# Spreading the last norm's rows in four quarters, and seeding both final row halves ahead of the last scatters, in a hybrid MoE kernel

## The chip, the cores and the metric

The kernel runs on one core of one Trainium2 chip. The metric is device time in microseconds (us), the median of a few runs. One further execution was taken by the hardware profiler; all rows below come from it. The engines are named as in the profile: PE (TensorE matmuls), PEld (its weight loads), DVE (VectorE), ACT (ScalarE), POOL (GpSimd), SP (SyncE, which issues the weight DMAs).

## What is computed

Two layers over 256 tokens of width 1024, float32. Layer 0 mixes tokens by a Conformer convolution, layer 1 by chunkwise retention with four heads. After each mixer comes a mixture of experts (MoE) in which every token goes to two of 32 experts of one chosen group. Every sub-layer is followed by a norm:

```python
for i in range(DEPTH):                       # DEPTH = 2
    mix = conformer_conv(x, ...) if i % 2 == 0 else retention(x, positions, ...)
    x = layer_norm(DEEPNORM_ALPHA * x + mix, ln1_g[i], ln1_b[i])
    ffn = hier_moe(x, ...)                   # sum over e of combine[:, e] * (silu(x @ w_gate[e]) * (x @ w_up[e])) @ w_down[e]
    x = layer_norm(DEEPNORM_ALPHA * x + ffn, ln2_g[i], ln2_b[i])
```

All 32 experts' weights (1024x512 twice and 512x1024 once per expert) are read in each layer, whatever the routing.

## The kernel before

**Stages.** Convolution, MoE of layer 0, retention, MoE of layer 1, output. In an MoE stage `experts` runs over 32 experts `e` and, inside each, over four steps `i` (0 to 3); a place in it is written (e, i) here. `gate_up(e, i)` multiplies the expert's gathered 64 token slots with a quarter of its gate and up weights: four matmuls, 8 records in the trace, since a matmul with fp32 operands leaves two records. `hidden(e)` after (e, 3) makes silu(gate) times up, on ACT and DVE. `turn(e)` transposes that on PE (tile `hT`). `down(es, kt)` multiplies with a quarter of the down weights of a pair of experts (tile `y`, again 8 records). `parts` scales and splits the result into a high and a low fp32r part (`yh`, `yl`), `places` builds the 0/1 matrix that puts slots back on tokens (`sp`, `s`), and `scatter` adds a pair's result to the tokens: eight one-pass matmuls, two token halves `tt` by two column halves `n` by high and low. For most pairs DVE then adds the PSUM tile to the tokens in `cur`.

**The end of a stage.** The last pairs are not added by DVE. `begin(tt)` seeds two PSUM tiles `fin` with `cur` itself, by a matmul of the identity with `cur` in fp32 operands, and the last scatters accumulate onto them; the norm then reads `fin`. Before, `begin(0)` stands at (30, 3) and `begin(1)` at (31, 3); the scatter of pair 14 at (31, 2) therefore goes into `fin` for token half 0 alone, and through DVE for half 1. Experts 30 and 31 are handled singly (numbers -2 and -1 in tile names).

**The norm's rows.** The last norm needs its scale and shift on all 128 partitions. `spread_rows` makes them from a 32-row tile `lnr`: 16 matmuls, each broadcasting one column of the identity, into four PSUM tiles, each copied out by ACT. Before, all four are made at one place, `ROWS_AT = (29, 0)`, after `run(29, 0)`.

**The order.** The order on every engine is the order of the code. The table `plan`, filled by `planned(e, q, ...)`, says which of down, turn, parts, place, scatter, begin follow the gate/up group at (e, q). `Weights` streams 1 MB weight pieces through a ring of SBUF tiles: SP issues a piece when a tile is free and an earlier transfer has landed. Within an expert the pieces come as gate and up (first half), down pieces where the plan has them, gate and up (second half).

**PSUM.** Eight tiles of 512 columns: four of tag `acc` (`acc1`: gate/up and down results), four of tag `sm` (`sm1`: transposes, gathers, places, scatters, rows, `fin`).

Of the kernel before, what the change touches and what calls it, by code (L numbers as in the profile page):

```python
# [10 lines left out]
F32 = mybir.dt.float32  # L11
F32R = mybir.dt.float32r
BF = mybir.dt.bfloat16
I32 = mybir.dt.int32
AF = mybir.ActivationFunctionType
OP = mybir.AluOpType
AX = mybir.AxisListType

P = 128
D = 1024  # L20
T = 256
KT = 8
DEPTH = 2
NE = 32
# [8 lines left out]
ONCE = {7: "split", 16: "hand", 17: "hand"}  # L33
T4 = 9
SPLIT = 4
ROWS_AT = (29, 0)
WARM = [11, 8, 8, 0, 2, 0, 1, 2]
YB = 2
TAPS_PE = [2, 2, 2, 2, 2, 2, 2, 14]
# [4 lines left out]
RW = 2 * DEPTH * KT  # L44
# [142 lines left out]
def trunk(ctx, tc, a, out):  # L187
    nc = tc.nc
    ET = mybir.EngineType
    V, S, G, PE = nc.vector, nc.scalar, nc.gpsimd, nc.tensor  # L190
# [15 lines left out]
    def sm1(name, dt=F32):  # L206
        return psum.tile([P, 512], dt, tag="sm", name=name, bufs=4)
# [10 lines left out]
    def planned(e, q, *steps):  # L218
        plan.setdefault((e, q), []).extend(steps)


    for p in range(NE // 2 - 1):
        e, both = 2 * p + 2, (2 * p, 2 * p + 1)
        planned(e - 1, 0, ("turn", e - 2))
        planned(e, 0, ("turn", e - 1))
        planned(e, 2, ("down", both, 0))
        planned(e, 3, ("down", both, 1))
        planned(e + 1, 0, ("down", both, 2))
        planned(e + 1, 1, ("down", both, 3), ("parts", p), *([("place", -2)] if p == NE // 2 - 2 else []))
        if p < NE // 2 - 2:  # L230
            planned(e + 2, 0, ("scatter", p))
    z = NE - 1
    planned(z - 1, 3, ("begin", 0))
    planned(z, 0, ("turn", z - 1))
    planned(z, 2, ("down", (z - 1,), 0), ("scatter", NE // 2 - 2), ("down", (z - 1,), 1), ("place", -1))
    planned(z, 3, ("begin", 1), ("down", (z - 1,), 2), ("down", (z - 1,), 3), ("part", -2), ("turn", z),
            *[("down", (z,), k) for k in range(4)], ("ahead", 2), ("part", -1), ("ahead", 4), ("scatter", -2),
            ("scatter", -1))

# [41 lines left out]
    lnr = consts.tile([RW, P], F32, name="lnr")  # L281
# [7 lines left out]
    part = cc[:, 259:260]  # L289
# [16 lines left out]
    ident = consts.tile([P, P], F32, name="ident")  # L306
# [13 lines left out]
    def cut(t):  # L320
        return [t[:, n:n + 512] for n in range(0, t.shape[1], 512)]
# [1 line left out]
    def row_bcast(src, n):  # L323
        return bass.AP(tensor=src.tensor, offset=src.offset, ap=[[0, P], [1, n]])

    def spread_rows(L, o):

        for n in range(4):
            ps = sm1(f"row{L}{n}")
            for k in range(4):  # L330
                q = L * 2 * KT + n * 4 + k
                PE.matmul(ps[:, k * P:(k + 1) * P], ident[:RW, q:q + 1].to_broadcast([RW, P]), lnr, start=True, stop=True)
            S.activation(o[:, n * 512:(n + 1) * 512], ps, AF.Copy)

    def layer_stats(tt, halves, name):
        st = small.tile([P, 2, 6], F32, tag="bst", name=name + "st")
# [306 lines left out]
    def halves(tt):  # L643
        return [cur[:, tt, n * 512:(n + 1) * 512] for n in range(2)]
# [286 lines left out]
    def moe(L, prev, next_front):  # L931
        with tc.tile_pool(name=f"moe{L}", bufs=1) as mp:
            x1h = mp.tile([P, 2, KT, P], F32R, tag="x1h", name="x1h")
            x1l = mp.tile([P, 2, KT, P], F32R, name="x1l")
            comb = mp.tile([P, 2, NE], F32, name="comb")
            posm = mp.tile([P, 2, NE], F32, name="posm")
            posT = mp.tile([NE, T], BF, name="posT")
            flag = mp.tile([1, 1], I32, name="flag")
            W.open(mp)
            with tc.tile_pool(name=f"exp{L}", bufs=1) as ep:  # L940
                norms(*prev, moe_front(L, x1h, x1l))
                W.more()
                route(L, ep, mark["lg"], comb, posm, posT, flag)
                fin = experts(L, mp, ep, x1h, x1l, comb, posm, posT, flag)
                W.room.update(own=0, split=0)
                norms([fin[0], fin[1]], *mark["ln2"], f"lnm{L}", next_front(), 4)
# [91 lines left out]
    def experts(L, mp, ep, x1h, x1l, comb, posm, posT, flag):  # L1038
# [91 lines left out]

        def places(pr):

            sp = sm1(f"sp{pr}")
            for j in range(2):
                e = 2 * pr + j if pr >= 0 else NE + pr
                PE.matmul(sp[j * CAP:(j + 1) * CAP, :T], identb[:NE, e:e + 1].to_broadcast([NE, CAP]), posT,  # L1136
                          start=True, stop=True)
            s0[pr] = ep.tile([P, T], F32R, tag="s0", name=f"s0{pr}", bufs=2)
            V.tensor_scalar(s0[pr], sp[:, :T], slot, None, op0=OP.is_equal)  # L1139
# [10 lines left out]
        def scatter(pr, on=None):  # L1150

            for tt in range(2):
                for n in range(2):
# [6 lines left out]
                    if not held:  # L1160
                        o = halves(tt)[n]
                        V.tensor_tensor(o, ps, o, op=OP.add)  # L1162

        def begin(tt):
            fin[tt] = [sm1(f"fin{tt}{n}") for n in range(2)]
            for n in range(2):
                PE.matmul(fin[tt][n], ident, halves(tt)[n], start=True, stop=False)

        def run(e, q):
            for what, *step in plan.get((e, q), ()):  # L1170
                if what == "down":
                    down(*step)
                elif what == "turn":
                    turn(*step)
                elif what == "begin":
                    begin(*step)
                elif what == "parts":
                    places(*step)
                    parts(*step)
                elif what == "place":  # L1180
                    places(*step)
                elif what == "part":
                    parts(*step)
                elif what == "ahead":
                    W.stop = len(pieces)
                    W.ahead(*step, pool=step[0] > 2)
                else:
                    scatter(*step, fin)

        def extra():  # L1190
# [5 lines left out]
            pair = [acc1(f"ov{n}") for n in range(2)]  # L1196
            with tc.If(rv > 0):
                overflow(L, x1h, x1l, comb, posm, wts, big, mid, row, pair)
        fin = {}
        W.stop = layers[L][1]  # L1200
        one_hots(0)
        warm(WARM[5])
# [2 lines left out]
        for e in range(NE):  # L1205
            for i in range(4):
                gate_up(e, i)
                if e == 0 and i == 0:
                    gather(0, range(2, 4))
                    turned()  # L1210
                if e == 0 and i == 3:
                    extra()
                    W.used(2)
                    for tt in range(2):
                        S.activation(cur[:, tt], cur[:, tt], AF.Copy, scale=ALPHA)
                if i == 3:
                    hidden(e)
                run(e, i)
                if e + 4 < NE and e % 4 == 1 and i == 0:
                    one_hots(e // 4 + 1)  # L1220
                if e + 2 < NE and e % 4 == 2:
                    gather(e // 4 + 1, [i])
                if (e, i) == ROWS_AT:
                    rows = mp.tile([P, 2048], F32, tag="x1h", name=f"rows{L}")
                    spread_rows(L, rows)
            if L == 0 and e == 3:
                mark["rot"] = rotary_tables()
            if L == 0 and e == 10:
                mark["rot"]()
        rows = cut(rows)  # L1230
# [74 lines left out]

    moe(0, conv(), ret_front)
    moe(1, retention(), out_front)


# [59 lines left out]
```

## Time and profile before

| | us |
|---|---|
| timed runs, median (lowest to highest) | 1306.99 (1303.9 to 1308.12), 3 runs |
| profiled execution, device time | 1302.16 |
| profiled execution, span of the trace | 1300.4 |
| PE busy in the span | 1253.6 (96%) |
| DVE / ACT / POOL busy | 488.2 / 334.3 / 139.4 |

PE's busy share includes records whose ends are modelled, and a matmul that stalls on weights is drawn stretched, so 96% is not 96% of useful work. Times in the rows are from the span's start. "xN" is the number of records merged in a row; what stands in brackets is the idle time of that engine just before the row and what ended it.

### The profile page before, as it was taken

What the parts mean: (1) busy time and instruction counts of PE and PEld (TensorE: products, weight loads), DVE (VectorE), ACT (ScalarE), POOL (GpSimd) and SP (SyncE); (2) the same over time, 40 slices, a digit from 0 to 9 for tenths busy, and PEclk for the clock granted to TensorE, in tenths of its full rate; (3) what the DMA queues carried; (4) which work ended last, traced back from release to release, by engine and by line L of the source; (5) the groups of instructions that cost most, each with busy time, mean ns of one, the idle gap of its engine ahead of it and who ended that gap; (6) DMA issues with size and microseconds to landing.
All of it is one profiled execution on the core that took longest, in us unless ns stands there. A gap on an engine that the chain in (4) does not pass through costs nothing.

```text
span 1300.4 us, 15536 instructions
## 1 busy us (share of the span) xinstructions
PE 1253.6 (96%) x6163; PEld 662.8 (51%) x6163; DVE 488.2 (38%) x859; ACT 334.3 (26%) x553; POOL 139.4 (11%) x165
## 2 busy tenths in 40 slices
PE   9989899999999999998999999899999999999996
PEld 7867444343443434434997788544443444434432
DVE  5987322223222222126666755413222232222224
ACT  4655321121111112113433543311111111111111
POOL 4881009100000000003130000000000000000000
PEclk9999799999999999999999999799999999999998
DMA  9935699999999999999655565699999999999992
GB/s 322 392 127 176 231 385 427 426 424 426 425 426 426 425 426 426 425 426 407 234 191 181 174 209 199 239 382 420 418 425 426 424 427 426 426 425 424 426 427 83
DMA packets 102391, 459.45 MB, mean 353 GB/s; under 512 B 8259, under 2 KB 25443, under 8 KB 59555
## 3 DMA queue, kind: packets, MB, share of 16 engines
q1 hardware_dynamic: 102082, 457.92, 87.3%
q8 instruction: 53, 0.87, 0.2%
q0 software_dynamic: 80, 0.26, 0.1%
q10 hardware_dynamic: 144, 0.15, 0.1%
q14 instruction: 32, 0.25, 0.1%
HBM read 457.25 MB, written 1.05 MB: 352 GB/s over the span
## 4 chain that ended last, share of the span: by engine, by line
PE 47%; DMA 38%; DVE 2%; ACT 1%; issue 0%; DVEq 0%; SPq 0%; ACTq 0%
DMA w<-in_moe_w_up_dram 21%; PE gu L1071 15%; DMA w<-in_moe_w_down_dram 14%; PE y L1126 7%; PE gp L1057 3%; DMA w<-in_moe_w_gate_dram 2%; PE vg L790 2%; PE vg L788 2%; PE vg L789 2%; PE sc L1158 2%; PE qk L771 1%; PE qk L770 1%; PE qk L768 1%; PE wo L656 1%; PE wo L657 1%; PE wo L658 1%
## 5 line engine op out<-in xcount | busy, mean ns | idle before, releaser
L1071 PE MATMUL gu<-w,xghi 128*64 128x512 f32 x1024 | 256.0, 614 | 2.6 <-DMA w<-in_moe_w_up_dram 1.4
L1126 PE MATMUL y<-w,h 128*64 128x512 f32 x960 | 240.4, 596 | 10.8 <-DMA w<-in_moe_w_down_dram 10.8
L1071 PE MATMUL gu<-w,xglo 128*64 128x512 f32 x1024 | 242.4, 599 | 0.0
L1082 DVE TENSOR_TENSOR h<-gl,gu 64x512 f32<-64x512 f32 x64 | 67.8, 1059 | 364.5 <-ACT gl L1080 364.5
L1126 PEld LDWEIGHTS y<-w,h 128*64 128x64 f32 x960 | 73.1, 138 | 156.9 <-issue 136.5
L1071 PEld LDWEIGHTS gu<-w,xglo 128*64 128x64 f32 x1024 | 70.1, 137 | 119.5 <-issue 110.9
L1071 PEld LDWEIGHTS gu<-w,xghi 128*64 128x64 f32 x1024 | 68.6, 139 | 114.0 <-issue 103.7
L143 DVE TENSOR_TENSOR l<-w,h 128x1024 fp32r<-128x1024 f32 x66 | 83.6, 1270 | 68.5 <-ACT h L142 66.9
L1080 ACT ACTIVATE gl<-gu 64x512 f32<-64x512 f32 x64 | 37.7, 589 | 243.7 <-PE gu L1071 243.6
L142 ACT ACTIVATE h<-w 128x1024 fp32r<-128x1024 f32 x72 | 75.7, 1058 | 88.1 <-PE vg L790 31.7
L1104 ACT ACTIVATE h<-hT 128x256 f32<-128x256 f32 x64 | 24.6, 385 | 270.8 <-PE hT L1101 153.7
L1162 DVE TENSOR_TENSOR cur<-sc,cur 128x512 f32<-128x512 f32 x116 | 72.1, 684 | 23.3 <-PE sc L1158 23.3
L1113 DVE COPY gsl<-hT 64x1 f32<-64x1 f32 x60 | 9.4, 156 | 174.6 <-ACT h L1104 174.1
L1057 PE MATMUL gp<-oh,x1h 128*128 128x256 f32 x256 | 59.0, 313 | 3.5 <-DVE route L1010 3.5
L1146 ACT ACTIVATE yh<-y,gsl 128x512 fp32r<-128x512 f32 x60 | 41.2, 687 | 80.5 <-PE y L1126 80.4
L1057 PEld LDWEIGHTS gp<-oh,x1h 128*128 128x128 f32 x256 | 40.5, 196 | 40.3 <-issue 39.3
L466 PE MATMUL pw<-xT,w 128*128 128x256 f32 x256 | 57.8, 381 | 1.6 <-DMA w<-in_conv_w_pw_dram 1.6
L499 POOL TENSOR_TENSOR gp<-gp,gt 128x256 f32<-128x256 f32 x76 | 56.3, 742 | 21.9 <-ACT gt L498 16.5
L143 POOL TENSOR_TENSOR l<-w,h 128x1024 fp32r<-128x1024 f32 x6 | 14.9, 2516 | 369.4 <-ACT h L142 369.4
L466 PEld LDWEIGHTS pw<-xT,w 128*128 128x128 f32 x256 | 48.2, 190 | 8.8 <-issue 2.4
L1057 PE MATMUL gp<-oh,x1l 128*128 128x256 f32 x256 | 52.6, 288 | 0.0
L1139 DVE TENSOR_SCALAR s<-sp,cc 128x256 fp32r<-128x256 f32 x30 | 14.5, 484 | 97.9 <-PE sp L1136 97.9
(319 smaller groups left out, 1582.7 us busy)
## 6 DMA issues: line engine op xcount, KB each, us to landing
w<-in_moe_w_up_dram SPq DMA_DIRECT2D x116, 1024.0 KB, 14.9
w<-in_moe_w_down_dram SPq DMA_DIRECT2D x112, 1024.0 KB, 17.1
w<-in_moe_w_gate_dram SPq DMA_DIRECT2D x106, 1024.0 KB, 14.7
w<-in_ret_w_qkvg_dram SPq DMA_DIRECT2D x24, 1024.0 KB, 13.2
w<-in_moe_w_gate_dram SPq DMA_DIRECT2D x44, 512.0 KB, 14.7
w<-in_moe_w_down_dram SPq DMA_DIRECT2D x32, 512.0 KB, 16.7
w<-in_moe_w_up_dram SPq DMA_DIRECT2D x24, 512.0 KB, 17.2
w<-in_conv_w_pw_dram SPq DMA_DIRECT2D x16, 512.0 KB, 6.3
```

The costliest lines, as they stand in the source:

```text
L142: self.nc.scalar.activation(hi, w, AF.Copy)
L143: (self.nc.gpsimd if pool else self.nc.vector).tensor_tensor(lo, w, hi.bitcast(F32), op=OP.subtract)
L466: PE.matmul(ps[:, 1 - g], w[g][:, kt], xT[:, kt], start=kt == 0, stop=kt == KT - 1)
L499: G.tensor_tensor(gps[c], gps[c], t, op=OP.add)
L788: PE.matmul(ps[tt], xh(kt)[:, ts], hi[:, k], start=kt == 0, stop=False)
L1057: PE.matmul(ps[:, k], src[:, tt, q * 2 + k], o[:, tt].rearrange("p e c -> p (e c)"), start=i == 0, stop=i == 3)
L1071: PE.matmul(gus[e][m * CAP:(m + 1) * CAP], l, w[i % 2 * 2 + k], start=kt == 0, stop=kt == KT - 1)
L1080: S.activation(gl, gu[:CAP], AF.Silu)
L1082: V.tensor_tensor(hs[e].rearrange("s k p -> s p k"), gl.rearrange("s (p k) -> s p k", k=4), gu[CAP:].rearrange("s (p k) -> s p k", k=4), o ...
L1126: PE.matmul(ys[pr][b][j * CAP:(j + 1) * CAP], hs[e][:, kt], wds[e][kt % 2][:, n * 512:(n + 1) * 512], start=kt == 0, stop=kt == 3)
L1146: S.activation(yh[:, n], ys[pr][n], AF.Copy, scale=g)
L1162: V.tensor_tensor(o, ps, o, op=OP.add)
```

## The change

Three things are moved or replaced, in both MoE stages.

1. `spread_rows` takes a quarter `n` and makes one PSUM tile of rows; the four quarters go to (27, 0), (27, 2), (28, 0) and (28, 2).
2. `begin` no longer multiplies with `cur` in fp32. A new step `seed(tt)` splits that half of `cur` into a high part (ACT copy to fp32r) and a low part (DVE subtraction) in SBUF, in the memory of the tile `x1l` that the gathers no longer need; `begin` accumulates both with an fp32r identity `identr`, which POOL makes once per stage. `seed(0)` stands at (30, 0), `seed(1)` at (30, 3) behind `begin(0)`.
3. `begin(1)` moves from (31, 3) to (31, 1), ahead of the scatter of pair 14, which now accumulates into `fin` for both token halves: two DVE additions go. The place tiles of experts 30 and 31 take PSUM tiles of tag `acc` instead of `sm`.

```diff
-ROWS_AT = (29, 0)
+ROWS_AT = [(27, 0), (27, 2), (28, 0), (28, 2)]
...
+        planned(e + 1, 1, ("down", both, 3), ("parts", p), *([("begin", 1), ("place", -2)] if p == NE // 2 - 2 else []))
...
-    planned(z - 1, 3, ("begin", 0))
+    planned(z - 1, 0, ("seed", 0))
+    planned(z - 1, 3, ("begin", 0), ("seed", 1))
...
-    planned(z, 3, ("begin", 1), ("down", (z - 1,), 2), ("down", (z - 1,), 3), ("part", -2), ("turn", z),
+    planned(z, 3, ("down", (z - 1,), 2), ("down", (z - 1,), 3), ("part", -2), ("turn", z),
...
-            sp = sm1(f"sp{pr}")
+            sp = (sm1 if pr >= 0 else acc1)(f"sp{pr}")
...
+        def seed(tt):
+
+            t = mp.tile([P, 2, 2, 512], F32R, tag="x1l", name=f"seed{tt}")
+            for n in range(2):
+                S.activation(t[:, 0, n], halves(tt)[n], AF.Copy)
+                V.tensor_tensor(t[:, 1, n], halves(tt)[n], t[:, 0, n].bitcast(F32), op=OP.subtract)
+            seeds[tt] = t
...
-                PE.matmul(fin[tt][n], ident, halves(tt)[n], start=True, stop=False)
+                for i in range(2):
+                    PE.matmul(fin[tt][n], identr, seeds[tt][:, i, n], start=i == 0, stop=False)
...
+        identr = ep.tile([P, P], F32R, name="identr")
+        G.tensor_copy(identr, ident)
...
-                if (e, i) == ROWS_AT:
-                    rows = mp.tile([P, 2048], F32, tag="x1h", name=f"rows{L}")
-                    spread_rows(L, rows)
+                if (e, i) in ROWS_AT:
+                    n = ROWS_AT.index((e, i))
+                    if n == 0:
+                        rows = mp.tile([P, 2048], F32, tag="x1h", name=f"rows{L}")
+                    spread_rows(L, rows, n)
```

PE in the second layer, kernel before: the end of expert 29's first step (the last down group of experts 26 and 27 at (29, 0), expert 28's transpose `hT`), the rows, and the gate/up group of (29, 1).

```order
L1126 MATMUL y_8630<-w_8509,h_8615 64x512
L1091 MATMUL hT_8664<-ident,h_8645 128x64 x4
L1101 MATMUL hT_8664<-comb,oh_8366 128x2 x2
L332 MATMUL row_8677<-lnr,ident 128x128 x4
L332 MATMUL row_8683<-lnr,ident 128x128 x4
L332 MATMUL row_8689<-lnr,ident 128x128 x4
L332 MATMUL row_8695<-lnr,ident 128x128 x4
L1071 MATMUL gu_8655<-w_8495,xghi_8441 64x512
```

PE at the same place of the changed kernel.

```order
L1126 MATMUL y_8663<-w_8523,h_8642 64x512
L1091 MATMUL hT_8703<-ident,h_8684 128x64 x4
L1101 MATMUL hT_8703<-comb,oh_8380 128x2 x2
L1071 MATMUL gu_8694<-w_8509,xghi_8455 64x512
L1071 MATMUL gu_8694<-w_8511,xghi_8455 64x512
```

The 16 row matmuls are gone from between the transpose and the gate/up group; the last of their four quarters now stands at (28, 2), in the changed kernel's PE order behind the first down group of the pair 26 and 27:

```order
L1126 MATMUL y_8662<-w_8471,h_8551 64x512
L1126 MATMUL y_8662<-w_8473,h_8642 64x512
L1126 MATMUL y_8663<-w_8471,h_8551 64x512
L1126 MATMUL y_8663<-w_8473,h_8642 64x512
L332 MATMUL row_8668<-lnr,ident 128x128 x4
L1071 MATMUL gu_8616<-w_8419,xglo_8456 64x512
```

Four of the 16 row matmuls stand there; the other three quarters stand in the same way behind (27, 0), (27, 2) and (28, 0).

PE around the last gate/up group of expert 31, before: `begin(1)` stands between that group and expert 30's down groups.

```order
L1071 MATMUL gu_8802<-w_8707,xglo_8442 64x512
L1167 MATMUL fin_8882<-cur,ident 128x512
L1167 MATMUL fin_8883<-cur,ident 128x512
L1126 MATMUL y-20_8852<-w_8715,h_8820 64x512 x4
L1091 MATMUL hT_8894<-ident,h_8880 128x64 x4
```

PE of the changed kernel where `begin(1)` now stands, at (31, 1), between the place matmuls of pair 14 and of expert 30.

```order
L1136 MATMUL sp_8858<-posT,identb 64x256
L1176 MATMUL fin_8869<-seed_8823,identr 128x512 x2
L1176 MATMUL fin_8870<-seed_8823,identr 128x512 x2
L1136 LDWEIGHTS identb
L1136 MATMUL sp-2_8875<-posT,identb 64x256
```

So expert 31's transpose follows its last gate/up group with one down group between them, where it had a begin and a down group before.

## Rows read from the trace of the kernel before

**Rows 1.** Busy time by stage: stretch, us, PE PEld DVE ACT POOL, PEclk, DMA share, GB/s.

```profile
1203.00:1232.00 29.00, 26.59 (x117) 9.68 (x116) 6.73 (x11) 3.32 (x6) 0.00 (x0) 1.00 1.01 427
...
1235.00:1240.00 5.00, 5.00 (x19) 2.82 (x19) 0.00 (x0) 1.20 (x3) 0.00 (x0) 0.50 1.02 422
...
1270.00:1274.00 4.00, 4.00 (x19) 1.85 (x16) 1.93 (x4) 0.20 (x1) 0.00 (x0) 1.00 0.45 188
```

**Rows 2.** SP's own waits, 1190 to 1260 us: us in total, times, longest.

```profile
SPq L127 <- DMA w<-in_moe_w_up_dram: 16.2, 9, 2.1
...
SPq L127 <- PE gu L1071: 0.2, 1, 0.2
```

**Rows 3.** PE's timeline, experts 27 to 29: start, us, instructions, idle before.

```profile
1202.95 1.94 PE L1071 MATMUL gu<-w,xghi 128*64 128x512 f32 x8
...
1219.81 1.47 PE L1126 MATMUL y<-w,h 128*64 128x512 f32 x5 [0.80 <-DMA w<-in_moe_w_down_dram]
...
1229.54 1.93 PE L1126 MATMUL y<-w,h 128*64 128x512 f32 x6 [1.45 <-DMA w<-in_moe_w_down_dram]
1231.40 0.46 PE L1091 MATMUL hT<-ident,h 64*128 64x64 f32 x4
```

**Rows 4.** PE's timeline in experts 30 and 31.

```profile
1252.72 1.89 PE L1071 MATMUL gu<-w,xglo 128*64 128x512 f32 x8
1254.44 1.89 PE L1126 MATMUL y<-w,h 128*64 128x512 f32 x8
...
1263.37 1.89 PE L1126 MATMUL y<-w,h 128*64 128x512 f32 x8
```

**Rows 5.** The chain that ended last, in order of time: start, us, what.

```profile
1232.39 4.71 PE row L332 x32
1237.11 3.61 PE gu L1071 x8
1240.72 2.33 PE y L1126 x8
...
1259.76 1.91 PE fin L1167 x4
...
1272.53 1.13 PE fin L1158 x4
1273.66 0.93 PE sc L1158 x4
...
1281.47 0.39 PE hT L1091 x4
```

**Rows 6.** Weight issues on SP (start, us) and, below each, us to landing.

```profile
1234.45 0.33 SPq L127 DMA_DIRECT2D w<-in_moe_w_down_dram  x1
w<-in_moe_w_down_dram SPq DMA_DIRECT2D x1, 1024.0 KB, 14.7
1240.62 0.33 SPq L127 DMA_DIRECT2D w<-in_moe_w_down_dram  x1
w<-in_moe_w_down_dram SPq DMA_DIRECT2D x1, 1024.0 KB, 18.3
```

**Rows 7.** The first layer's end: the rows in the chain, and a weight issue.

```profile
546.24 4.64 PE row L332 x32
...
554.49 0.33 SPq L127 DMA_DIRECT2D w<-in_moe_w_down_dram  x1
```

**Rows 8.** ACT and DVE in the tail, from their timelines.

```profile
1233.51 0.60 ACT L333 ACTIVATE rows<-row 128x512 f32<-128x512 f32 x1 [0.70 <-PE row L332]
...
1249.28 2.49 DVE L1162 TENSOR_TENSOR cur<-sc,cur 128x512 f32<-128x512 f32 x4 [0.67 <-PE sc L1158]
...
1278.36 1.04 DVE L1082 TENSOR_TENSOR h<-gl,gu 64x512 f32<-64x512 f32 x1 [2.01 <-ACT gl L1080]
```

**Rows 9.** Busy time by stage, columns as in Rows 1: retention, the second MoE.

```profile
700.00:720.00 20.00, 20.00 (x84) 14.78 (x83) 13.69 (x22) 7.15 (x10) 0.00 (x0) 1.00 0.56 193
...
880.00:1160.00 280.00, 279.21 (x1372) 115.37 (x1372) 73.13 (x119) 45.55 (x81) 0.00 (x0) 1.00 1.01 425
```

More of the change, by code (lines that the diff above doesn't have):

```diff
@@ L228, in trunk @@
         planned(e + 1, 0, ("down", both, 2))
-        planned(e + 1, 1, ("down", both, 3), ("parts", p), *([("place", -2)] if p == NE // 2 - 2 else []))
+        planned(e + 1, 1, ("down", both, 3), ("parts", p), *([("begin", 1), ("place", -2)] if p == NE // 2 - 2 else []))
         if p < NE // 2 - 2:
@@ L324, in row_bcast, with spread_rows @@
         return bass.AP(tensor=src.tensor, offset=src.offset, ap=[[0, P], [1, n]])
[L326 to L333, printed above, removed]
+    def spread_rows(L, o, n):
+        ps = sm1(f"row{L}{n}")
+        for k in range(4):
+            q = L * 2 * KT + n * 4 + k
+            PE.matmul(ps[:, k * P:(k + 1) * P], ident[:RW, q:q + 1].to_broadcast([RW, P]), lnr, start=True, stop=True)
+        S.activation(o[:, n * 512:(n + 1) * 512], ps, AF.Copy)
     def layer_stats(tt, halves, name):
@@ L933, in moe @@
             x1h = mp.tile([P, 2, KT, P], F32R, tag="x1h", name="x1h")
-            x1l = mp.tile([P, 2, KT, P], F32R, name="x1l")
+            x1l = mp.tile([P, 2, KT, P], F32R, tag="x1l", name="x1l")
             comb = mp.tile([P, 2, NE], F32, name="comb")
@@ L1174, in run @@
                     turn(*step)
+                elif what == "seed":
+                    seed(*step)
                 elif what == "begin":
@@ L1198, in extra @@
                 overflow(L, x1h, x1l, comb, posm, wts, big, mid, row, pair)
-        fin = {}
+        fin, seeds = {}, {}
+        identr = ep.tile([P, P], F32R, name="identr")
+        G.tensor_copy(identr, ident)
         W.stop = layers[L][1]
```

## The prediction

> **What bounds the kernel now.** PE's 96% on the page says little, since stalled matmuls are drawn stretched. I read the second MoE's end first, as a table by stage. The DMA share is 1.01 to 1.02 at 422 to 427 GB/s, and 0.45 in the slice from 1270 to 1274 [rows 1]: the weight stream runs without a hole until the last weight has landed. Then SP's own waits from 1190 us, to see what gates its issues: earlier landings (nine waits for up weights, 16.2 us; those for gate and down read alike), hardly PE (0.2 us) [rows 2]. Hence **landing times are set from the side of DMA**: PE can be early or late by some microseconds without moving them.
>
> PE's timeline next: it waits for weights through expert 28 and into 29, for the last time until 1229.54 (1.45 us), and never again [rows 3]. Behind that wait the chain shows 32 records of the spread rows, and then PE's own work to the end. One oddity: the gate/up group behind the rows takes 3.61 us and the down group 2.33, where their kind takes 1.72 from start to start [rows 4, 5]. The table says why: PE's granted clock is 1.00 through all the waits up to 1232 and 0.50 (1.2 GHz) from 1235 to 1240, so it fell in the rows [rows 1].
>
> **The change, part by part** (second layer's times; the profiled execution took 1302.16 us, 1300.4 of it the span, the median of the timed runs is 1306.99: I take the difference from the one and lay it on the other).
>
> *Rows out of (29, 0).* 4.71 us in the chain, and the slow groups behind them: 1.9 + 0.6 = 2.5 [rows 5]. PE would be 7.2 us earlier behind them.
>
> *Rows into (27, 0), (27, 2), (28, 0), (28, 2).* The same work in quarters, 4.71/4 = 1.18 us four times. What hides it? From 1202.95 to 1231.40 PE takes 28.45 us [rows 3]. Its work there is eight gate/up and four down groups at 1.72 to 1.77 (21.0), a scatter of eight one-pass matmuls (1.13 + 0.93 = 2.06) and some 0.6 of small things: 23.7 us [rows 4, 5]. So 4.75 us are waits, though only 0.80 + 1.45 and less than 0.2 more are drawn as idle [rows 3]. The first three quarters stand where PE does not wait; they make it late for waits that come later, so the sum counts: 4.71 to hide in 2.4 to 4.75. PE is 0 to 2.3 late at 1231.4. I take 0, since the sum of work rests on spacings of unstalled groups and the drawn idle on modelled ends. What the cover lacks goes into the next item. Each quarter also takes one PSUM tile and one ACT copy of 0.60 [rows 8]; ACT has 3.32 of 29 us busy there [rows 1].
>
> *What is late next.* PE, early by up to 7.2, runs into weights again. Expert 29's first down piece is issued at 1234.45 and takes 14.7: it lands at 1249.15. Before, PE came to it at 1254.44 + 0.43 (the group's second matmul) = 1254.87, so it can be at most **5.7** early. The first seed then saves 0.9 (below), 6.6 in all, but the second down piece is issued at 1240.62 and takes 18.3: 1258.92. Before, PE came to it at 1263.37 + 0.43 = 1263.80, so at most **4.9** early [rows 4, 6]. These two new waits (7.2 − 5.7 = 1.5, 6.6 − 4.9 = 1.7 us) swallow up to 3.2 us of lateness from the quarters without moving the end. Six more pieces follow at 2.4 us each, to about 1271 to 1274; the work that wants the last of them comes after 1281 before and after 1276 now, so none binds.
>
> *Seeds.* A begin is two matmuls with fp32 operands, four records, 1.91 us; after, four one-pass matmuls, for which the nearest rows are the scatter's: 1.13 and 0.93 for four [rows 5]. I take 1.0: 0.9 saved each. The first saving is eaten by the 1258.92 landing; the second, now at about 1265, comes behind it and counts. Beside PE stand four ACT copies and four DVE subtractions per layer, nearest rows 0.60 and 2.49/4 = 0.62 [rows 8]: about 2.4 on ACT, 2.5 on DVE. The first pair may use 1251.77 (end of DVE's additions) to 1259.76, the second the 8 us between the two begins; a pair needs 1.2 + 0.6 behind its wait, so both are hidden by the gate/up and down groups between. Behind the second pair's wait on ACT is queued expert 30's copy out of its transpose, which PE reaches two groups later. Without cover a pair would put up to 1.9 us on PE. POOL gets one cast per layer, and is 11% busy.
>
> *New waits.* The second begin needs two PSUM tiles; the latter is that of the place matmul just ahead, which one DVE operation empties while the begin's first half runs: 0 to 0.6, I take 0.2. And no begin of 1.91 now stands between expert 31's last gate/up and its transpose. DVE ends that expert's hidden values at 1278.36 + 1.04 = 1279.40; the transpose, before at 1281.47, would now be due at 1279.56 on the same scale: it just meets them, 0 to 0.5, I take 0.1 [rows 5, 8].
>
> **Sum per layer:** 4.9 + 0.9 − 0.3 = **5.5 us**.
>
> *First layer.* The same rows 686 us earlier: 4.64 for the rows, and the binding down piece issued at 554.49, its landing time again 18.3 [rows 7]. So 5.5 once more. Is it kept? Retention is PE's (busy 20.00 of 20.00, DMA share 0.56), so it starts and ends earlier, and the second MoE's stream, 1.01 from 880 on, starts earlier with it [rows 9]. I see nothing tied to absolute time. **Total 11.0**: 1302.16 → 1291.2 for the profiled execution, 1306.99 → **1296.0**.
>
> *A rule against this.* The clock fell in a stretch in which PE counts as busy 4.71 of 4.71 us. The Trainium skill (TensorE: Matmul & The Clock Gate, Part 1) says that throttled is the default state and that activity releases it. By that rule the busy rows should not have lost the clock, and the waits for weights ahead of them would be to blame; the trace does not agree, with 1.00 through all of those waits. By the rule the sum would be rival C's, by the row it is 5.5.
>
> **Rivals.**
> A. *Only one layer's gain arrives,* because the second stream hangs on something that is not shifted. Nothing seen for it; rows 9 against it. 1306.99 − 5.5 = 1301.5.
> B. *Weights do not bind:* the stream gets earlier where PE does, and PE's whole saving counts, 7.2 + 1.8 per layer: 1289.0. Against it: rows 2.
> C. *The clock falls behind the new waits,* which stand late: behind 1258.9 nothing swallows the price, 2.5 per layer as it was: 3.0 left, 1301.0. For it: 1.5 and 1.7 us of waiting close together. Against it: the waits before cost no clock.
> D. *Slower: each quarter halves the clock as the lump did.* 2.5 to 3.4 us a time (3.4 if 6.8 us at half clock are all dense work), four times, plus 4.7 of rows less 4.75 of cover: 10.0 to 13.6 late at 1231.4. The lump had cost 7.2 and the seeds give 1.8: 1.0 to 4.6 slower per layer, 1309 to 1316. It decides from three quarters on (late by more than 7.2 + 1.8 − 0.3 = 8.7); one is swallowed by the waits at 1249 and 1259. Against it: a quarter stands between dense groups, the lump stood alone.
> E. *The quarters miss the waits,* so the change does not do what it says: PE 2.3 late at 1231.4. The new waits take 3.2, so 1296.0 still.
>
> **How the numbers follow.** Forecast with E 0.72; A 0.07; B 0.05; C 0.09; D 0.07. The forecast's own range per layer is 4.6 (stalls 0.6 and 0.5, the seed at 1.13) to 7.0 (no stalls, the binding landing earlier by half a piece, 1.2): 1293.0 to 1297.8, widened by the timed runs' spread of about 2. With A and C inside the upper end, 1291.5 to 1302.0 leaves out B, D and tails, under 2 in 10. 0.3% (3.9 us) is about what a measurement can tell from no change. Faster than that is below 1303.1: forecast, B, most of A and C, 0.87. Within it: the rest of A and C and a mild D, 0.08. Slower: 0.05.
>
> **What would show it.** After: no lump behind (29, 0), and clock 1.00 to the end of the experts; four groups of 8 row records at about 1.2 us in experts 27 and 28; PE waits for down weights in expert 30's second half and expert 31's start, each ended by a landing; begins of about 1.0; the end of the first MoE 5 to 6 us earlier and of the second 10 to 12. No wait for weights behind expert 29 would make the binding term wrong (B); a granted 0.50 in experts 27 to 31 points to D or C; a first-layer gain gone by the first experts of the second layer, to A.

## The result and the profile after

| | before | after | ratio, 95% interval |
|---|---|---|---|
| timed runs, median (lowest to highest), us | 1305.45 (1302.41 to 1308.12), 6 runs | 1292.73 (1289.8 to 1297.98), 6 runs | 0.993 (0.9907 to 0.9952) |
| a second comparison | 1301.62 (1298.29 to 1305.37), 12 runs | 1293.71 (1291.16 to 1297.74), 7 runs | 0.9943 (0.9923 to 0.9963) |
| profiled execution, device time (span) | 1302.16 (1300.4) | 1292.11 (1290.4) | |

The kernel is faster, by 0.7% and 0.6%, with both intervals below 1: 12.7 us in the first comparison and 7.9 in the second, 10.05 between the two profiled executions. Predicted were 11.0, and 1296.0 for a time of 1292.73.

The yardstick of everything below is the end of a MoE stage: the start of the first down group of expert 31 (tile `y-1`, line 1126). In the second layer 17.7 us follow it to the end of the span, before and after. PE's timeline of the kernel before, first and second layer (the number behind `y-10` counts tiles):

```profile
596.55 3.65 PE L1126 MATMUL y-10_4184<-w,h 128*64 128x512 f32 x16 [0.49 <-ACT h L1104]
...
1282.69 1.51 PE L1126 MATMUL y-10_8907<-w,h 128*64 128x512 f32 x6 [0.49 <-ACT h L1104]
```

After, the chain of work that ended last (start, us, what), second layer and then first:

```profile
1235.40 18.32 DMA w<-in_moe_w_down_dram
...
1253.77 1.93 PE y L1126 x6
...
1260.14 1.31 PE fin L1176 x4
...
1272.65 3.68 PE y-10_8931 L1126 x16
```

```profile
554.33 18.35 DMA w<-in_moe_w_down_dram
...
591.60 3.68 PE y-10_4196 L1126 x16
```

The end comes 4.95 us earlier in the first layer and 10.04 in the second. Before, the last weight transfer in the chain landed ahead of the lump of rows, and behind it stood the lump and then PE's own work [rows 5]; now, in both layers, the last transfer in it is the second half of expert 29's down weights. From its landing to expert 31's down group it is 18.92 us in both layers (1253.72 to 1272.65, 572.68 to 591.60). Before it was 1258.95 to 1282.69, 23.74, and 572.82 to 596.55, 23.73 [landings: rows 6, 7]. So 4.81 us of the gain lie behind that landing in either layer, 9.6 of the 10.05.

PE's timeline after, experts 27 and 28: the first and the last of the four quarters (two like them at 1204.49 and 1211.61), and expert 28's transpose:

```profile
1197.73 1.15 PE L332 MATMUL row<-lnr,ident 32*128 32x128 f32 x8
...
1217.99 1.15 PE L332 MATMUL row<-lnr,ident 32*128 32x128 f32 x8
...
1226.15 0.46 PE L1091 MATMUL hT<-ident,h 64*128 64x64 f32 x4
```

Each quarter takes 1.08 us from start to start, and no idle time is drawn between the first of them and 1240: the waits of [rows 3] are used up. Expert 28's transpose comes at 1226.15 instead of 1231.40, 5.25 earlier. The landing moved by the same 5.23 (1258.95 to 1253.72), so PE is not late there: this shift is what the first layer and the retention stage handed on.

The same timeline further on:

```profile
1242.12 1.02 PE L1126 MATMUL y<-w,h 128*64 128x512 f32 x2
1244.05 1.47 PE L1126 MATMUL y<-w,h 128*64 128x512 f32 x5 [0.91 <-DMA w<-in_moe_w_down_dram]
...
1249.31 1.21 PE L1176 MATMUL fin<-seed,identr 128*128 128x512 f32 x4
...
1252.22 1.02 PE L1126 MATMUL y<-w,h 128*64 128x512 f32 x2
1253.77 1.93 PE L1126 MATMUL y<-w,h 128*64 128x512 f32 x6 [0.53 <-DMA w<-in_moe_w_down_dram]
1255.63 0.46 PE L1091 MATMUL hT<-ident,h 64*128 64x64 f32 x4
...
1258.02 1.89 PE L1126 MATMUL y<-w,h 128*64 128x512 f32 x8
1259.84 0.29 PE L1136 MATMUL sp<-posT,identb 32*64 32x256 bf16 x2
...
1269.40 1.89 PE L1126 MATMUL y-20_8884<-w,h 128*64 128x512 f32 x8
1271.36 0.46 PE L1091 MATMUL hT<-ident,h 64*128 64x64 f32 x4
```

The two new waits stand where the prediction put them, at expert 29's first and second down piece, each ended by a landing. By the spacing of the groups they take 1.9 us (1242.12 to 1249.31 is 7.19, where it was 5.25) and 1.6 us (1252.22 to 1255.63 is 3.41, where it was 1.82); 0.91 and 0.53 of that are drawn as idle. The first begin takes 1.14 us to the next group's start at 1250.45, the second 1.31 by the chain.

Busy time by stage after (columns as in [rows 1]), one row over the four quarters and both new waits:

```profile
1190.00:1262.00 72.00, 70.57 (x345) 28.84 (x342) 19.03 (x32) 14.16 (x25) 0.00 (x0) 1.00 1.01 426
```

Granted clock 1.00 throughout this stretch, where it had been 0.50 from 1235 to 1240.

In the first layer PE was late. Ahead of the quarters the granted clock fell in a down group behind a wait for weights, with no rows near it, and the group took 3.4 us where the stalled one above takes 1.86 (PE's timeline, with expert 28's transpose, and the table by stage):

```profile
484.25 3.50 PE L1126 MATMUL y<-w,h 128*64 128x512 f32 x6 [1.42 <-DMA w<-in_moe_w_down_dram]
...
546.68 0.46 PE L1091 MATMUL hT<-ident,h 64*128 64x64 f32 x4
```

```profile
484.00:488.00 4.00, 3.75 (x10) 0.99 (x10) 0.00 (x0) 0.00 (x0) 0.00 (x0) 0.57 1.01 426
```

So expert 28's transpose stands 26.00 us ahead of the landing at 572.68, where it stood 27.58 ahead before (545.24 to 572.82): PE was 1.6 us late. It lost only 0.35 us at expert 29's first piece and waited for the second as above. The end behind the landing is 18.92 us all the same.

### The profile page after: what moved, and what is told of

It is laid out like the page before. It is cut to its first block, busy times and chain, and to the rows that moved or that the text cites. A ratio compares the mean times of both kernels' runs of the same rounds, so it can differ in the third digit from the quotient of the medians.

```text
span 1290.4 us, 15546 instructions
## 1 busy us (share of the span) xinstructions
PE 1246.8 (97%) x6163; PEld 659.6 (51%) x6163; DVE 490.5 (38%) x863; ACT 338.7 (26%) x561; POOL 139.9 (11%) x167
## 4 chain that ended last, share of the span: by engine, by line
PE 60%; DMA 25%; DVE 2%; ACT 1%; issue 0%; DVEq 0%; SPq 0%; ACTq 0%
PE gu L1071 22%; DMA w<-in_moe_w_up_dram 11%; DMA w<-in_moe_w_down_dram 11%; PE y L1126 10%; PE gp L1057 4%; PE sc L1158 3%; DMA w<-in_moe_w_gate_dram 2%; PE vg L788 2%; PE vg L790 2%; PE vg L789 2%; PE hT L1091 1%; PE qk L771 1%; PE qk L770 1%; PE qk L768 1%; PE wo L656 1%; PE wo L657 1%
## 5 line engine op out<-in xcount | busy, mean ns | idle before, releaser
L1071 PE MATMUL gu<-w,xghi 128*64 128x512 f32 x1024 | 250.5, 606 | 1.9 <-DMA w<-in_moe_w_up_dram 1.0
L1162 DVE TENSOR_TENSOR cur<-sc,cur 128x512 f32<-128x512 f32 x112 | 69.5, 683 | 19.0 <-PE sc L1158 19.0
```

The costliest lines, as they stand in the source:

```text
L1071: PE.matmul(gus[e][m * CAP:(m + 1) * CAP], l, w[i % 2 * 2 + k], start=kt == 0, stop=kt == KT - 1)
```

## The experiments

Theory L: behind the quarters the landing of expert 29's second down half sets the end, in whatever way PE comes to be early. Theory W, its rival: what is taken off PE comes off the end, one for one. Theory P explains why the end behind the landing is 0.4 us longer than forecast: matmuls into the two halves of the PSUM partitions run side by side.

Single profiles differ by some microseconds in the stages ahead of the MoE's end, where the clock falls now in one place and now in another: in the first layer the landing of expert 29's second down half comes anywhere from 569.68 to 578.11 us in the kernels below. So the starts that the expectations name for the first layer were mostly missed (592.19 measured for 591.6 without rows, 593.84 for 589.2 with one piece less), and they cannot tell the theories apart. The experiments are compared by one distance, from the landing of expert 29's second down half (its row of issue plus the time to landing, which the trace holds to the hundredth) to expert 31's first down group. Two kernels, marked *, have another order of the down groups.

| kernel | first layer, us | second layer, us |
|---|---|---|
| before | 23.73 | 23.74 |
| before, second profile | 22.04 | 22.11 |
| after | 18.92 | 18.92 |
| after, second profile | 18.95 | 18.92 |
| rows in quarters, old begins | 19.41 | 19.41 |
| new seeds, old lump | 19.05 | 22.41 |
| no rows at all | 18.92 | 18.92 |
| lump at (28, 2) | 18.92 | 18.93 |
| one weight piece less | 18.94 | 18.90 |
| begin(1) late | 18.63 | 18.61 |
| high part of the seeds alone | 18.68 | 18.66 |
| one group's matmuls reordered | 18.98 | 18.97 |
| down groups of the last pair later* | 16.79 | 16.81 |
| the same and begin(1) ahead of them* | 16.18 | 16.22 |

### One half of the change alone

Rows in four quarters on the kernel before, `begin` unchanged:

```diff
-ROWS_AT = (29, 0)
+ROWS_AT = [(27, 0), (27, 2), (28, 0), (28, 2)]
...
```

> Only the rows are moved (four quarters at (27,0), (27,2), (28,0), (28,2)); begins stay as in the kernel before. Theory L (the landing of expert 29's second down half sets the end): per layer the group that waits for it ends at landing + 1.86 us instead of at 1265.19, so 4.4 us per layer and 8.7 in all; the start of expert 31's down group at about 592.2 in the first layer (before 596.55, after the whole change 591.60). Theory W (what is taken off PE comes off the end): 4.71 + 2.5 = 7.2 per layer, 14.4 in all. PE should wait for weights in experts 30 and 31 under L and not under W.

Measured: 1294.78 us, ratio 0.9938 (0.9913 to 0.9964). The distance is 19.41 in both layers, 0.49 over that of the whole change and 4.32 under that of before: 8.6 us over both layers, where theory L said 8.7 and W 14.4. The first begin with fp32 operands, 1.91 us in its old form, costs nothing here, since PE waits for the landing behind it; only the second counts.

The seeds alone, rows as a lump at (29, 0):

```diff
-ROWS_AT = [(27, 0), (27, 2), (28, 0), (28, 2)]
+ROWS_AT = (29, 0)
...
+                    for n in range(4):
+                        spread_rows(L, rows, n)
...
```

> Only the seeds and begins are changed; all four quarters of the rows stay together at (29,0). Theory L: PE is late behind the lump, no landing binds, so both begins count: 0.75 + 0.6 = 1.3 us per layer, 2.7 in all, more than the 1.1 by which the whole change should exceed the rows alone. If the parts simply added up, whole minus rows alone would be the same 1.1 as here. The clock falls in the lump as before (0.50 for some 6.8 us).

Measured: 1301.06 us, ratio 0.998 (0.996 to 0.9999). The medians differ by 0.6 us where theory L had 2.7; the executions of this kernel spread over 9 us. In the second layer the distance falls by 1.33 us, as two cheaper begins would make it. But in the first it falls by 4.68, to 19.05, with the lump still in its old place. PE's timeline of this kernel shows why, first layer above, second below:

```profile
551.39 3.83 PE L332 MATMUL row<-lnr,ident 32*128 32x128 f32 x32
555.15 1.94 PE L1071 MATMUL gu<-w,xghi 128*64 128x512 f32 x8
...
558.73 0.29 PE L1136 MATMUL sp<-posT,identb 32*64 32x256 bf16 x2
...
1233.79 5.50 PE L332 MATMUL row<-lnr,ident 32*128 32x128 f32 x32
1239.21 3.55 PE L1071 MATMUL gu<-w,xghi 128*64 128x512 f32 x8
...
1244.41 0.29 PE L1136 MATMUL sp<-posT,identb 32*64 32x256 bf16 x2
```

```profile
551.00:556.00 5.00, 5.00 (x40) 4.35 (x42) 0.31 (x2) 2.77 (x5) 0.00 (x0) 1.00 1.02 423
...
1233.00:1239.00 6.00, 6.00 (x40) 5.91 (x39) 0.31 (x2) 2.17 (x4) 0.00 (x0) 0.72 1.01 419
```

The lower pair is the table by stage (clock third from the end of a row). The same 32 records in the same place kept the full clock in one layer and lost it in the other. From the lump's start to the place matmul it is 7.34 us at full clock and 10.62 with the fall: the rows themselves cost 3.76, the fall 3.3. So nearly half of the 7.2 us that the prediction took off PE was not the rows' work but the clock. And in the first layer, where only the fall was gone, the end came within 0.13 us of the whole change. That speaks for L and against W: between expert 28's transpose and the landing PE had 3.76 us more to do than in the whole change, and the end lost 0.13 by it.

### How regular the fall is

The kernel before, unchanged, profiled again:

> The kernel before, unchanged, profiled a second time, to see how regular the clock's fall in the lump of spread rows is. In the first profile the clock fell in the lump of both layers (rows 4.65 us from start to start, the gate/up group behind them 3.5, the down group 2.6); in the kernel with the new seeds and the old lump it fell in the second layer alone (rows 5.42 us there, 3.76 in the first), and the start of expert 31's down group stood 49.99 us behind expert 28's transpose where it fell and 46.70 where it did not. Theory F (the fall comes with the lump, one layer without it was the exception): 0.50 in both layers, expert 31's down group 51.3 us behind expert 28's transpose in both. Theory G (it comes and goes by the layer): full clock in at least one layer, rows 3.8 us there, and expert 31's down group 47.9 us behind the transpose (51.3 less the 3.4 that the fall costs), 3.4 us off that execution's end.

Measured: 1300.37 us. PE's timeline, second layer, and the table by stage behind the lump (1.00 up to 1236):

```profile
1232.14 3.83 PE L332 MATMUL row<-lnr,ident 32*128 32x128 f32 x32
1235.90 3.14 PE L1071 MATMUL gu<-w,xghi 128*64 128x512 f32 x8
...
1241.18 0.29 PE L1136 MATMUL sp<-posT,identb 32*64 32x256 bf16 x2
```

```profile
1236.00:1240.00 4.00, 4.00 (x12) 1.22 (x14) 0.00 (x0) 0.60 (x1) 0.00 (x0) 0.57 1.03 426
```

Neither theory had this: the clock falls in both layers, but for half as long and only behind the rows. From the lump's start to the place matmul it is 9.04 us; the fall costs 1.7. So in six layers with the lump at (29, 0) the fall cost 3.3 us in three, 1.7 in two and nothing in one. How much the change gives thus depends on the execution of the kernel before: 4.8 us per layer, 3.15 (22.07 − 18.92), or some 1.5 (23.73 − 3.3 − 18.92). That the two timed comparisons differ (12.7 and 7.9 us) fits this, but the clock of the timed runs is known only as a mean, so it is argued, not shown.

### The rows' price where they now stand

The rows left out, a constant in their place:

```diff
-                    spread_rows(L, rows, n)
+                        G.memset(rows, 1.0)
```

> The changed kernel with the rows left out on PE and ACT: the tile of scale and shift is filled with ones by POOL, so scale and shift of the second norms are left out of the computation. Theory L: the quarters are wholly hidden, so the end stays where the whole change puts it, within 0.5 us per layer (start of expert 31's down group 591.6 in the first layer), and PE shows its waits in experts 28 and 29 again, some 4.7 us in all. Theory W: 4.7 us per layer earlier still (586.9).

Measured: 1292.78 us, one run; the distance is 18.92 twice, that of after. The four quarters cost nothing: where they were, PE waits instead. From expert 26's transpose to expert 28's, second layer, it is 29.34 us with them (1196.81 to 1226.15) and 29.34 without (1197.39 to 1226.73).

The rows as one lump, but at (28, 2):

```diff
-ROWS_AT = [(27, 0), (27, 2), (28, 0), (28, 2)]
+ROWS_AT = (28, 2)
...
```

> The changed kernel with all four quarters of the rows together at (28,2), ahead of the waits but not spread. If the lump itself lowers the clock: 0.50 for one or two stretches of 3.4 us right in or behind it, PE up to 2.5 us late at expert 28's transpose, and by theory L (the landing sets the end) swallowed by the later waits, so expert 31's down group starts at 591.6 to 592.0 in the first layer. If the waits for weights ahead of the old lump were at fault: clock 1.00 here, the same end. By theory W (PE's work sets the end) a slow clock puts its 2.5 on the end of each layer.

Measured: 1296.76 us, one run, beside 1305.59 for before. PE's timeline and the issue and landing of expert 29's second down half, second layer:

```profile
1221.03 4.25 PE L332 MATMUL row<-lnr,ident 32*128 32x128 f32 x32
...
1233.44 0.46 PE L1091 MATMUL hT<-ident,h 64*128 64x64 f32 x4
...
1257.56 2.78 PE L1126 MATMUL y<-w,h 128*64 128x512 f32 x8
...
1277.30 3.65 PE L1126 MATMUL y-10_8931<-w,h 128*64 128x512 f32 x16 [0.49 <-ACT h L1104]
```

```profile
1240.03 0.33 SPq L127 DMA_DIRECT2D w<-in_moe_w_down_dram  x1
w<-in_moe_w_down_dram SPq DMA_DIRECT2D x1, 1024.0 KB, 18.3
```

The clock fell here too in the second layer (0.57 from 1224 to 1228). No wait of PE is drawn from 1172 us to the lump, so the waits ahead of the old lump are not what the fall needs; in the first layer the same lump kept the full clock. In the second, expert 28's transpose stands 24.9 us ahead of the landing instead of 27.6: PE is 2.6 us late. It no longer waits at the first down piece, and the group at 1257.56, with a landing at 1258.37 inside, still ends where it would have ended. The distance is 18.93. So the price of rows and fall is swallowed by the waits that the change itself opens; rival D was harmless for one fall.

### Moving the landing itself

One weight piece less in the stream: the second half of expert 29's up weights is not loaded, and its gate weights stand in for it.

```diff
-  for w in (wg, wu)
+  for w in ((wg,) if (e, q) == (29, 2) else (wg, wu))
...
```

> The changed kernel with one weight piece of 1 MB not loaded per layer: expert 29's second half of up weights is left out, the gate's second half is used in its place. PE's work is the same. Theory L: all later landings are 2.45 us earlier and the end of each MoE is 2.2 to 2.5 us earlier (expert 31's down group at about 589.2 in the first layer). Theory W: no change (591.6).

Measured: 1292.59 us, one run. Measured from the landing of expert 27's second down half, which lies ahead of the missing piece, expert 31's down group comes 46.22 and 45.95 us later in the two layers, against 48.49 and 48.40 in after: 2.3 and 2.5 earlier, and the pieces of the stream come 2.4 apart. From the landing of expert 29's second half, which moved with it, it is 18.94 and 18.90, as in after. PE's own work is unchanged, and the end followed the landing: L, and the opposite of W. (Its device time shows less of it, as the stages ahead of the MoE took longer in that execution.)

### What lies behind the landing

Why 18.92 and not less? The begin with half of its matmuls, the low part of the seeds left out:

```diff
-                for i in range(2):
-                    PE.matmul(fin[tt][n], identr, seeds[tt][:, i, n], start=i == 0, stop=False)
+                PE.matmul(fin[tt][n], identr, seeds[tt][:, 0, n], start=True, stop=False)
```

> The changed kernel with the low part of the seeds left out of the begins (two matmuls each instead of four). Theory L: what the first begin saves (0.5) is eaten by the landing behind it, the second's counts: 0.5 us earlier per layer. Theory W: 1.0 per layer.

Measured: 1294.04 us, one run; distance 18.68 and 18.66. Two matmuls less in this begin, at 0.23 us each from start to start, give only 0.25 us where theory L had 0.5, for the reason that PE's timeline draws in the second begin:

```profile
1262.88 0.50 PE L1175 MATMUL fin<-seed,identr 128*128 128x512 f32 x1 [0.16 <-DVE s L1139]
```

The begin waits for DVE to empty the tile of the place matmul ahead. Then `begin(1)` back at (31, 3), with its seed at (31, 2):

```diff
-    planned(z - 1, 3, ("begin", 0), ("seed", 1))
+    planned(z - 1, 3, ("begin", 0))
...
-... ("down", (z - 1,), 1), ("place", -1))
+... ("down", (z - 1,), 1), ("place", -1), ("seed", 1))
-    planned(z, 3, ("down", (z - 1,), 2), ...
+    planned(z, 3, ("begin", 1), ("down", (z - 1,), 2), ...
```

> The changed kernel with the second begin back at (31,3), in one-pass parts; its seed is made behind the last scatter, whose second token half goes through DVE again. If the second begin pays for a PSUM tile that DVE still empties at (31,1): it takes 1.1 here against 1.31 and 1.32, and the end is 0.2 us earlier per layer, unless the seed arrives late: then PE waits at the begin for DVE and the end is later by that wait. Rival: the early place itself gains, and the end is some 1 us later per layer.

Measured: 1288.6 us, one run; distance 18.63 and 18.61, 0.3 less than after.

```profile
1264.85 1.19 PE L1176 MATMUL fin<-seed,identr 128*128 128x512 f32 x4
1265.97 1.94 PE L1126 MATMUL y-20_8877<-w,h 128*64 128x512 f32 x8
1267.84 0.46 PE L1091 MATMUL hT<-ident,h 64*128 64x64 f32 x4
```

The begin takes 1.12 instead of 1.31, the place matmuls ahead share a start, and expert 31's transpose comes 1.87 behind the down group's start instead of 1.96. So the move to (31, 1) cost 0.3 us of the seeds' gain per layer.

Theory P: one group with the order of its matmuls changed, so that neighbours write the same half of the partitions.

```diff
-            for n in range(2):
-                for e in es:
+            order = [(n, e) for n in range(2) for e in es]
+            if pr == NE // 2 - 2 and kt == 3:
+                order = [(n, e) for e in es for n in range(2)]
+            for n, e in order:
```

> The changed kernel, with the last down group of the pair 28 and 29 issued expert by expert instead of alternating between the two experts, whose results lie in the two halves of the PSUM partitions. Theory P (matmuls of the two halves run at the same time, so a group that stalls between them loses that): this group takes 3.4 us from start to start instead of 1.72 and the end is 1.7 later per layer. Rival: every record costs its 0.215 whatever its neighbour, 1.72, and the end does not move.

Measured: 1295.48 us, one run. The reordered group, first layer:

```profile
579.58 1.94 PE L1128 MATMUL y<-w,h 128*64 128x512 f32 x8
581.45 0.29 PE L1138 MATMUL sp<-posT,identb 32*64 32x256 bf16 x2
```

1.87 us from start to start, against 1.82 (1258.02 to 1259.84) in after: the theory falls in the form in which it was put. What stays of it is seen inside the groups of after. The table by stage, of line 1126 alone; xN is the number of matmul records under way in a slice. The first three rows are the group that waits for the landing, the last two the next, unstalled one:

```profile
1252.55:1253.05 0.50, 0.50 (x2) 1.00 1.04 442
...
1254.30:1254.60 0.30, 0.30 (x4) 1.00 0.97 410
...
1255.15:1255.45 0.30, 0.30 (x2) 1.00 0.97 410
...
1258.50:1258.80 0.30, 0.30 (x4) 1.00 1.03 437
...
1259.35:1259.70 0.35, 0.35 (x4) 1.00 0.94 398
```

A record's modelled span reaches into the next, so a half that works counts as two, and four mean that both halves work. In an unstalled group they do to the end. In the stalled one, expert 28's half works alone ahead of the landing (x2), then both, then expert 29's alone again (x2). So each half of the PSUM partitions is a chain of its own: expert 29's two matmuls, 4 records of 0.43, are all still to come when its piece lands, and take 1.86 to the transpose (1253.77 to 1255.63), as long as the whole group unstalled. In the reordered kernel the halves worked side by side just the same, with four records in each slice of the group, although their matmuls were no neighbours. The Trainium skill (TensorEngine Tiling (Array Packing), Tiling Modes) says that different tiles of the array can load weights and multiply in parallel; here the records of the two halves agree.

### Later down groups

If the landing binds, the work of the pair 28 and 29 should stand later, with other work in the wait. First the down groups one step later:

```diff
-        planned(e, 2, ("down", both, 0))
+        last = p == NE // 2 - 2
+        planned(e, 3 if last else 2, ("down", both, 0))
...
-        planned(e + 1, 0, ("down", both, 2))
+        planned(e + 1, 1 if last else 0, ("down", both, 2))
...
```

> The changed kernel with the down groups of the pair 28 and 29 one place later each where they wait for weights: (30,2) to (30,3) behind the gate/up group there, and (31,0) to (31,1). The order of the weight pieces is the same, so are the landings. Theory L: the group that waited 1.5 us finds its piece landed, the second wait falls to some 0.3 plus the cost of a restart; 2.2 us per layer, 4.4 in all less than the changed kernel. Theory W: PE's work is the same, no change.

Then also `begin(1)` ahead of the down groups at (31, 1), and the scatter of pair 14 and its places ahead of expert 30's:

```diff
-        planned(e + 1, 1, ("down", both, 3), ("parts", p), *([("begin", 1), ("place", -2)] if p == NE // 2 - 2 else []))
+        planned(e + 1, 1 if last else 0, *([("begin", 1)] if last else []), ("down", both, 2))
+        planned(e + 1, 1, ("down", both, 3), ("parts", p))
...
-    planned(z, 2, ("down", (z - 1,), 0), ("scatter", NE // 2 - 2), ("down", (z - 1,), 1), ("place", -1))
+    planned(z, 2, ("scatter", NE // 2 - 2), ("place", -2), ("down", (z - 1,), 0), ("down", (z - 1,), 1), ("place", -1))
...
-            sp = (sm1 if pr >= 0 else acc1)(f"sp{pr}")
+            sp = (sm1 if 0 <= pr < NE // 2 - 2 else acc1)(f"sp{pr}")
```

> As e8, with the second begin ahead of the down group that waits at (31,1), the scatter of pair 14 ahead of expert 30's first down group at (31,2), and the place tiles in the other PSUM tag. The begin then fills the wait and finds its PSUM tiles free: 3.0 us per layer, 6.0 in all less than the changed kernel by theory L; theory W: no change but the begin's 0.2 per layer.

The kernel after ran beside both, as the control:

> The changed kernel itself, beside the two that follow: 0.7 to 0.9% under the kernel before.

| | median, us | ratio to before, 95% interval |
|---|---|---|
| after | 1293.71 | 0.9943 (0.9923 to 0.9963) |
| down groups later | 1289.02 | 0.9909 (0.9885 to 0.9934) |
| the same, begin(1) ahead of them | 1286.72 | 0.9894 (0.9871 to 0.9916) |

Both medians lie below that of the change, but only the second's interval stands apart from it. Off the distance the two orders take 2.1 and 2.7 us in each layer, where theory L had 2.2 and 3.0 and theory W next to nothing. PE's timeline of the second, where the two waits had been:

```profile
1240.61 3.85 PE L1127 MATMUL y<-w,h 128*64 128x512 f32 x16
1244.39 1.19 PE L1177 MATMUL fin<-seed,identr 128*128 128x512 f32 x4
1245.51 2.13 PE L1072 MATMUL gu<-w,xghi 128*64 128x512 f32 x8
...
1250.07 1.20 PE L1177 MATMUL fin<-seed,identr 128*128 128x512 f32 x4
1251.20 3.65 PE L1127 MATMUL y<-w,h 128*64 128x512 f32 x16
...
1255.01 2.43 PE L1072 MATMUL gu<-w,xglo 128*64 128x512 f32 x8
```

No wait is drawn any more, both begins take 1.12 to 1.13, and what is left shows as stretched gate/up groups (2.06 and 2.36 instead of 1.77): up weights of expert 31 land inside them, at 1245.66 and 1255.46. So PE still meets the stream there.

## Why the prediction held, point by point

**The sign and the size** were right: 11.0 forecast, 10.05 between the profiled executions, 12.7 and 7.9 between the medians. 11.0 (ratio 0.9916) lies inside the first interval and just outside the second. That 11.0 comes so close to 10.05 is in part luck: both rest on the first profile of before, in which the clock fell for long in both layers. Against its second profile the distances give 3.1 and 3.2 us per layer.

**Landings are set from the side of DMA**: right. From the landing of expert 27's second down half to that of expert 29's it is 29.48 and 29.46 us before (first and second layer) and 29.57 and 29.47 after, though PE's order between them changed and PE came 1.6 us later in the first layer.

**The quarters are hidden**: right, shown by the kernel without rows (18.92 either way). 4.75 us of waits were the right cover for 4.3 us of quarters (4 times 1.08), at full clock. In the first layer, where the clock's fall at 484 had made PE 1.6 us late, the new waits took the rest.

**7.2 us off PE**: the sum was right, its reading as a fixed price was not. Of it, 3.3 belong to the clock's fall, which was as long in the second layer of the seeds-only kernel, half as long in the second profile of before and absent once. The prediction took the clock's fall as part of the lump; the runs show that it comes with it in most layers, at different lengths.

**4.9 as the binding term** is the first step that was mis-sized. The prediction let PE want expert 29's piece 0.43 us behind the group's start, at 1263.80, and start again from there. But the second matmul belongs to the other half of the partitions and starts with the group: PE wanted the piece at 1263.37, and after a stall this half's whole chain still follows. The term is 1263.37 − 1258.95 = 4.4. The first piece shows the same: 1254.44 − 1249.15 = 5.3, and the wait took 7.2 − 5.3 = 1.9 where 1.5 was forecast. The end behind the landing shows it (1.86 to the transpose, where 1.29, six records at 0.215, and the transition would have followed from the prediction's view).

**0.9 less 0.3 for the second begin** is the second. Measured are 1.92 to 1.31, so 0.6: an unstalled begin takes 1.12 to 1.14 where 1.0 was taken, and the stall on DVE's emptying is the 0.2 that the prediction priced. The place matmuls now apart take 0.13 more, the transpose of expert 31 comes 0.09 later behind its down group (0.1 was forecast), the stalled group costs 0.09 (0.05 from the landing to its start, 0.04 over 1.82), and the fp32 begin's transition of 0.1 is gone: 0.6 − 0.13 − 0.09 − 0.09 + 0.1 = 0.4. Both terms together: 4.4 + 0.4 = 4.8 per layer instead of 5.5, which is the 4.81 measured.

**The first layer the same**: right, 4.81 in either. The retention stage handed it on: from expert 31's down group in the first layer to expert 28's transpose in the second it is 634.85 us before and 634.55 after (635.89 and 636.59 in the second profiles). So rival A is out, as that transpose is 5.25 earlier. The remaining 0.4 of the 10.05 lie in other stages.

**Rivals.** B (weights do not bind) is out by the chain and by the experiment with one piece less. C (the clock falls behind the new waits) and D (at each quarter) did not come: 1.00 through both. The rule of the Trainium skill that the prediction weighed (TensorE: Matmul & The Clock Gate, Part 1: throttled is the default, activity releases it) speaks for C, since every wait would put the clock at risk; the trace kept the full clock through 0.91 and 0.53 us of drawn waits, as it had through those of [rows 3]. But it did not always: in the first layer of the same trace it fell behind 1.42 us of wait. Of 44 waits of 1.3 us or more ahead of a down group of the MoE stages, in the fourteen profiles, five were followed at once by a clock of 0.50. So the prediction's argument against C, that waits cost no clock, held in its rows and is no rule.

The lump of rows remains a likely cause beside them: it lost the clock in six of eight layers, once with no wait ahead, while the waits at its old place with no rows behind them kept 1.00 in both layers of the kernel without rows. Why dense rows lose it at all, and for such different lengths, stays open: nothing that PE did ahead of the lump differs visibly between the two layers of the seeds-only kernel. E (PE late at expert 28's transpose) came in the first layer alone, by 1.6 us and through the clock; as it said, the new waits took that.

## What to carry to other kernels

When work is taken off an engine, follow it to the next transfer that it will wait for, and size the gain by that landing; here 4.4 of 7.2 us could arrive, and whatever else was done ahead of the landing, a lump at (28, 2), quarters or nothing, left the end where it was. The next step is then to put later work into the wait: moving two down groups, a begin and a scatter took a further 2.7 us off each layer. A price read from one profile of a stretch at half clock is to be checked in a second profile, as part of it may belong to the execution.

## What the runs showed that was not expected

- The same 32 row records at the same place took 3.76, 4.71 and 5.42 us, by the granted clock: full to their end, half in their last part, half earlier. The groups behind them lost up to 1.9 us each.
- The clock also fell with no rows near: five times in a down group right behind 1.3 to 1.4 us of waiting for weights, which made PE 1.6 to 1.7 us late. In the kernel after it cost nothing at the end, since the later waits took it.
- Matmuls into the two halves of the PSUM partitions run as two chains side by side, in whatever order they stand in the code: four matmuls of 128x512 against 64 columns take 1.82 us (1.87 reordered). A group that stalls for one half's operand needs 1.86 from the landing, as much as the whole group.
- A lump with a fall of the clock ahead of a wait for weights cost nothing at the end: PE 2.6 us late at one transpose, 18.93 against 18.92 behind the landing.
